# Transposed softmax weights of the first mixer's heads written into the PSUM bank of the small sums

## The chip, the cores and the metric

The kernel runs on one NeuronCore of a Trainium2 chip. The engines that matter are TensorE (PE in the profile; its weight loads have a row of their own, PEld), VectorE (DVE), ScalarE (ACT) and GpSimd (POOL). SyncE (SP) issues nearly all transfers from HBM. The results of TensorE land in PSUM, which has 8 banks of 128 partitions by 512 fp32 values. The metric is device time in microseconds of one execution; lower is better.

## The reference

One inference step of a two-layer diffusion backbone of width 2048 for two groups of 128 tokens: context tokens, and latent tokens that also attend to 128 cached context keys. Layer 0 has a mixer with two kinds of heads side by side, layer 1 another mixer; each is followed by a gated ConvFFN. A modulation vector per group and sub-layer (`silu(cond) @ w_ada`) gives shift, scale and gate. The change lies in layer 0's mixer alone:

```python
def mixer_ab(h, ...):                       # cut to what matters
    proj = h @ w_in
    qb = rmsnorm(8 query heads of 128, g_qn)            # grouped-query heads, 2 key heads
    qa = rmsnorm(q_lat, g_q) @ w_q_up                   # 8 latent heads of 128 + 64
    kv = ckv_all @ w_kv_up                              # their keys and values
    s  = q @ k.T * scale                                # 128 queries x 128 (group i) or 256 (group ii) keys
    out = softmax(s) @ v                                # 16 heads
    return concat(out) @ w_out
```

## The kernel before, in words

All activations stand transposed: features over the 128 partitions, the 256 tokens of both groups along the free axis. Every fp32 product is made exact enough by halves: each weight block is cast to a high half `wh` on ACT (L248), the rest `wl` is subtracted on DVE (L249), and three products (`wh` with the high half of the activations, `wl` with it, `wh` with their low half) are accumulated per block in a bank called `acc`. A product of a weight block therefore waits for its load, its cast and its subtraction.

The 8 banks of PSUM are given out by name: three `acc`; one `ada` for the sums of the modulation; three `att` for the attention; and one `misc` (function `bank`), which holds the small sums of the norms and their spread over the partitions. A name with several banks is a ring: who takes the next one waits until the last reader of its former content is done.

The stage of the heads takes from about 214 to 350 us of the span. It goes through four rounds (the loop over `h`). A round has three products with `w_q_up` (two latent queries, called `qn`, and their rotary part), the norms of two further grouped-query heads (`gqa_query`: a square on ACT, a sum of two 128x1 multiplications into `misc`, `rstd` with DVE L219 and a power on POOL L222, a scale on POOL L1238, a rotation on DVE L858 to L861), two grouped-query heads (`gqa`), two products with `w_kv_up` for keys, the values, and a pair of latent heads (`mla_pair`). Here G0 to G7 are the grouped-query heads and M0 to M7 the latent ones, in the order G0 G1 M0 M1, G2 G3 M2 M3 and so on.

What a head does is in `scores` and `head_ab`: scores into an `att` bank; two maxima on DVE (L867, L868); their negative and its scaling on POOL (L872, L873); two exponentials on ACT (L875), which also give the sums; a reciprocal on DVE (L903) and two multiplications that normalise `p` (L904, L905). Then `transposed`: three transposes of 128x128 on PE into one bank and a copy `pT` on ACT (L884). Then the three products with the values into another `att` bank, which are split in halves into `hx` (ACT L248, DVE L249).

Beside this runs side work for the modulation. `Deep` (L525) multiplies blocks of `w_ada` with the condition on DVE and sums them: two products of 128x1024 for each block, in tiles called `block` and `kvb`, each with a single home, so that the next load (SP L522) starts when the second product of the block before is done. On PE, `sum_rows` sums other blocks (`araw`, two buffers) into `ada`.

The order of the instructions on each engine is not written out. A scheduler lays it out beforehand along a simulated timeline in which waits for banks count; it may put any ready instruction first, other than those that `keep_order` holds in their written order (the side work and some others). So a changed bank can change the order on every engine, and that order is then fixed: an instruction that waits holds all those behind it on its engine.

Of the kernel before, what the change touches and what calls it, by code (L numbers as in the profile page):

```python
# [18 lines left out]
P = 128  # L19
# [75 lines left out]
def step_kernel(ctx: ExitStack, tc: tile.TileContext, A: dict):  # L95
# [34 lines left out]
    ppool = {}  # L130
# [6 lines left out]
    def nm(s):  # L137
        uid[0] += 1
        return f"{s}_{uid[0]}"

    def T_(pl, shape, tag, dt=F32, bufs=None):
        kw = {} if bufs is None else {"bufs": bufs}
        return pl.tile(shape, dt, tag=tag, name=nm(tag), **kw)
# [81 lines left out]
    def bank():  # L225
        return T_(pmisc, [P, 512], "misc")
# [20 lines left out]
    def split(out_hi, out_lo, src, pin=lambda i: i):  # L247
        pin(act.copy(out_hi, src))  # L248
        pin(dve.tensor_tensor(out=out_lo, in0=src, in1=out_hi.bitcast(F32), op=ALU.subtract))  # L249
# [614 lines left out]
    def softmax_parts(s, mx, sums, rs, const, p, pin=lambda i: i):  # L864

        nmx = T_(small, [P, 2], "nmx")
        pin(dve.tensor_reduce(out=mx[:, 0:1], in_=s[:, 0:T], axis=AX.X, op=ALU.max))  # L867
        pin(dve.tensor_reduce(out=mx[:, 1:2], in_=s[:, T:3 * T], axis=AX.X, op=ALU.max))  # L868
        if rs is None:
            pool.tensor_scalar(out=nmx, in0=mx, scalar1=-const, scalar2=None, op0=ALU.mult)  # L870
        else:
            pool.tensor_scalar(out=nmx, in0=mx, scalar1=-1.0, scalar2=None, op0=ALU.mult)  # L872
            pool.tensor_tensor(out=nmx, in0=nmx, in1=rs, op=ALU.mult)  # L873
        for g, c in ((0, slice(0, T)), (1, slice(T, 3 * T))):
            act.activation(p[:, c], s[:, c], AF.Exp, bias=nmx[:, g:g + 1],  # L875
                           scale=const if rs is None else rs[:, g:g + 1],
                           accum_out=sums[:, g:g + 1])

    def transposed(pl, p):
        pt = T_(ppool["att"], [P, 512], "att", bufs=3)  # L880
        for b in range(3):
            pe.transpose(pt[:, b * T:(b + 1) * T], p[:, b * T:(b + 1) * T], ident)
        o = T_(pl, [P, 3 * T], "pT", bufs=2)
        act.copy(o, pt[:, :3 * T])  # L884
        return o
# [10 lines left out]
    def head_ab(pl, s, rs, v, hx, c):  # L896

        mx = T_(small, [P, 2], "mx")
        sums = T_(small, [P, 2], "sums")
        p = T_(pl, [P, 3 * T], "p", bufs=3)  # L900
        softmax_parts(s, mx, sums, rs, None, p)
        rec = T_(small, [P, 2], "rec")
        dve.reciprocal(out=rec, in_=sums)  # L903
        dve.tensor_scalar(out=p[:, :T], in0=p[:, :T], scalar1=rec[:, 0:1], scalar2=None, op0=ALU.mult)  # L904
        dve.tensor_scalar(out=p[:, T:], in0=p[:, T:], scalar1=rec[:, 1:2], scalar2=None, op0=ALU.mult)  # L905
        yield
        yield
        pT = transposed(pl, p)
        yield
        o = T_(ppool["att"], [P, 512], "att", bufs=3)  # L910
        pe.matmul(o[:, 0:T], v(0), pT[:, 0:T], start=True, stop=True)
        pe.matmul(o[:, T:NT], v(1), pT[:, T:2 * T], start=True, stop=False)
        pe.matmul(o[:, T:NT], v(2), pT[:, 2 * T:], start=False, stop=True)
        split(hx[:, c, :NT], hx[:, c, NT:2 * NT], o[:, :NT])


    def mixer_ab(hx, beside):
        l = 0
        with tc.tile_pool(name="ab", bufs=1) as ab:
# [297 lines left out]
            with tc.tile_pool(name="abh", bufs=1) as hp:  # L1217
# [24 lines left out]
                def gqa(h):  # L1242
                    k = kg[:, h // 4]
                    return head_ab(hp, scores(qb[:, h], k), rsb[:, h], lambda b: vg[:, b, h // 4], o, 8 + h)
# [18 lines left out]
                def mla_pair(h, qr, kn, vm):  # L1263
                    s = [T_(ppool["att"], [P, 512], "att", bufs=3) for i in range(2)]
                    for g, ks in KEYS:
                        for i in range(2):
                            pe.matmul(s[i][:, ks], qn[h + i][:, g * T:(g + 1) * T], kn[i][:, ks],
                                      start=True, stop=False)
                        for i in range(2):
                            half = slice(64 * i, 64 * i + 64)  # L1270
                            m = pe.matmul(s[i][:, ks], qr[half, g * T:(g + 1) * T], kr[half, ks],
                                          start=False, stop=True)
                            if i:
                                keep_order(m)
                    for i in range(2):
                        start(head_ab(hp, s[i], rsm, lambda b, i=i: vm[:, b, i], o, h + i))
# [66 lines left out]
    def mixer_c(cp, hx, W, ready, st):  # L1343
# [70 lines left out]
        def attend(h, q, k, v):  # L1414
# [24 lines left out]
            yield  # L1439
            yield  # L1440
            pT = transposed(cp, pj[0])
            yield
            o = T_(ppool["att"], [P, 512], "att", bufs=3)
# [337 lines left out]
```

## Time and profile before

| | |
|---|---|
| time, median of 3 runs | 2304.97 us (2304.84, 2304.97, 2305.27) |
| profiled execution, its span | 2305.7 us (the page gives no other time of it) |
| busy in the whole span | PE 2275.9 us (99%), DVE 1885.6 us (82%), ACT 1195.7 us (52%), POOL 188.1 us (8%) |
| stage of the heads, 214 to 356 us: busy of 142 us | PE 135.66, DVE 114.95, ACT 73.47, POOL 25.90 |
| PE's granted clock in that stage | 0.98 of full speed |

The profiled execution is 0.7 us longer than the median of the timed runs. The page's chain of waits is the work that ended last, followed back from the end of the program; its timelines give each instruction's start and duration and, in brackets, the idle time before it and who ended that. A multiplication of fp32 operands (scores, sums S, sums into `ada`) stands as two records in the profile where the program has one instruction.

### The profile page before, as it was taken

The numbers are of one execution on the slowest core, as the hardware profiler recorded it, in microseconds if no ns is written. First come the engines' busy times: TensorE is split into PE (matmuls) and PEld (weight loads), VectorE is DVE, ScalarE is ACT, GpSimd is POOL, SyncE is SP. The second block draws the span as 40 slices with busy tenths as digits, with TensorE's granted clock in tenths as the row PEclk, the third lists the DMA queues.
The fourth block names the chain that finished last, engine by engine and source line by source line (L and its number), as shares of the span: only waits on it lengthen the run. The fifth ranks groups of instructions, "written<-read, shape, count | busy, mean of one in ns | idle before, by whom it ended". The sixth has DMA issues, their size and how long they took to land.

```text
span 2305.7 us, 47484 instructions
## 1 busy us (share of the span) xinstructions
PE 2275.9 (99%) x19496; PEld 2182.1 (95%) x19496; DVE 1885.6 (82%) x2973; ACT 1195.7 (52%) x1959; POOL 188.1 (8%) x238
## 2 busy tenths in 40 slices
PE   8999999999999999999999999999999999999998
PEld 6788878999999999999999999999999999999998
DVE  4667979989999999999978988898899965666654
ACT  4345555665553355555575455457555434555543
POOL 0002111300000000001130001023000000000011
PEclk9999999999999999999999999999999999999999
DMA  9987888777777777777788888776667755555553
GB/s 376 367 343 293 326 311 338 288 277 264 262 255 291 291 272 260 272 258 258 288 293 293 318 322 310 267 268 229 246 256 262 264 200 189 199 191 194 198 189 126
DMA packets 100122, 617.15 MB, mean 268 GB/s; under 512 B 10752, under 2 KB 18880, under 8 KB 33344
## 3 DMA queue, kind: packets, MB, share of 16 engines
q1 hardware_dynamic: 99904, 614.11, 72.2%
q8 instruction: 153, 2.51, 0.4%
q14 instruction: 65, 0.53, 0.1%
HBM read 609.32 MB, written 4.75 MB: 266 GB/s over the span
## 4 chain that ended last, share of the span: by engine, by line
PE 93%; DVE 3%; DMA 2%; issue 1%; POOL 1%; ACT 1%; SPq 0%; DVEq 0%; ACTq 0%; POOLq 0%
PE acc L110 86%; PE ada L110 3%; PE att L110 2%; DVE wl L249 1%; DVE hx L525 1%; DMA more<-w_ada 1%; PE att L113 1%; DMA raw<-w_out_c 0%; PE misc L110 0%; DMA araw<-w_ada 0%; DMA kvb<-w_ada 0%; POOL dev L807 0%; PE ada L113 0%; DVE rope L858 0%; ACT wh L248 0%
## 5 line engine op out<-in xcount | busy, mean ns | idle before, releaser
L110 PE MATMUL acc<-hx,wh 128*128 128x256 f32 (+1 forms) x7264 | 1255.2, 278 | 4.2 <-ACT wh L248 1.7
L248 ACT CAST wh<-raw 128x1024 fp32r<-128x1024 f32 (+1 forms) x834 | 796.6, 967 | 869.8 <-PE acc L110 736.6
L249 DVE TENSOR_TENSOR wl<-raw,wh 128x1024 fp32r<-128x1024 f32 (+1 forms) x834 | 925.4, 1126 | 246.9 <-ACT wh L248 240.2
L110 PEld LDWEIGHTS acc<-hx,wh 128*128 128x128 f32 x7264 | 1099.8, 188 | 23.2 <-ACT wh L248 8.1
L110 PE MATMUL acc<-hx,wl 128*128 128x256 f32 (+1 forms) x3632 | 1007.8, 278 | 5.3 <-DVE wl L249 5.1
L110 PEld LDWEIGHTS acc<-hx,wl 128*128 128x128 f32 x3632 | 684.5, 188 | 9.5 <-DVE wl L249 6.9
L110 PE MATMUL acc<-g,wh 128*128 128x256 f32 x2816 | 478.8, 276 | 0.0
L110 PEld LDWEIGHTS acc<-g,wh 128*128 128x128 f32 x2816 | 424.0, 188 | 0.0
L110 PE MATMUL acc<-g,wl 128*128 128x256 f32 x1408 | 388.1, 276 | 0.0
L473 DVE CUSTOM_DVE_ANT_0 junk<-araw,condb 128x2048 f32<-128x2048 f32 x128 | 294.4, 2300 | 0.0
L110 PEld LDWEIGHTS acc<-g,wl 128*128 128x128 f32 x1408 | 264.2, 188 | 0.0
L211 POOL TENSOR_TENSOR sqacc<-sqacc,sq 128x256 f32<-128x256 f32 x62 | 71.5, 1154 | 1491.1 <-ACT sq L207 1490.9
L110 PE MATMUL acc<-hxc,wh 128*128 128x256 f32 (+1 forms) x1056 | 189.3, 281 | 0.0
L110 PEld LDWEIGHTS acc<-hxc,wh 128*128 128x128 f32 x1056 | 161.9, 188 | 1.8 <-issue 1.7
L110 PE MATMUL acc<-hxc,wl 128*128 128x256 f32 (+1 forms) x528 | 146.9, 278 | 0.0
L110 PEld LDWEIGHTS acc<-hxc,wl 128*128 128x128 f32 x528 | 99.6, 189 | 0.2
L110 PE MATMUL acc<-wh,hxc 128*128 128x256 f32 (+1 forms) x512 | 95.0, 283 | 0.5 <-DVE nt L818 0.5
L1531 ACT ACTIVATE cv<-acc,convw 128x256 f32<-128x256 f32 x169 | 94.1, 557 | 0.0
L525 DVE CUSTOM_DVE_ANT_0 hx<-block,condb 128x1024 fp32r<-128x1024 f32 x65 | 79.3, 1221 | 7.3 <-DMA block<-w_ada 6.8
L1537 DVE SCALAR_TENSOR_TENSOR cv<-acc,convw,cv 128x254 f32<-128x254 f32 x169 | 81.1, 480 | 3.2
L843 DVE SCALAR_TENSOR_TENSOR x<-acc,mod,x 128x128 f32<-128x128 f32 x190 | 57.3, 344 | 31.6 <-PE acc L110 31.6
L110 PEld LDWEIGHTS acc<-wh,hxc 128*128 128x128 f32 x512 | 79.4, 188 | 3.4 <-issue 2.5
(263 smaller groups left out, 1800.4 us busy)
## 6 DMA issues: line engine op xcount, KB each, us to landing
raw<-w_up SPq DMA_DIRECT2D x176, 1024.0 KB, 4.8
araw<-w_ada SPq DMA_DIRECT2D x136, 1024.0 KB, 6.0
raw<-w_down SPq DMA_DIRECT2D x88, 1024.0 KB, 4.8
raw<-w_in_c SPq DMA_DIRECT2D x48, 1024.0 KB, 6.9
block<-w_ada SPq DMA_DIRECT2D x41, 512.0 KB, 6.8
raw<-w_in_ab SPq DMA_DIRECT2D x18, 1024.0 KB, 9.1
raw<-w_out_ab SPq DMA_DIRECT2D x16, 1024.0 KB, 7.9
raw<-w_out_c SPq DMA_DIRECT2D x16, 1024.0 KB, 7.1
```

Of the source, the lines that this page charges most:

```text
L110: return self.placed(nc.tensor.matmul(*a, **kw))
L113: return self.placed(nc.tensor.transpose(*a, **kw))
L211: eng.tensor_tensor(out=st["acc"], in0=st["acc"], in1=sq, op=ALU.add)
L248: pin(act.copy(out_hi, src))
L249: pin(dve.tensor_tensor(out=out_lo, in0=src, in1=out_hi.bitcast(F32), op=ALU.subtract))
L473: keep_order(dve.tensor_tensor_reduce(out=T_(feat["pool"], [P, D], "junk"), in1=feat["row"][:, c], in0=feat["raw"].rearrange("p g n -> p ( ...
L525: keep_order(dve.tensor_tensor_reduce(out=self.junk, in0=self.raw, in1=self.row[:, c].rearrange("p (g n) -> p g n", g=2), scale=1.0, scala ...
L843: dve.scalar_tensor_tensor(out=x[:, c, s], in0=ps[:, s], scalar=mod[:, l, 3 * which + 2, c, g:g + 1], in1=x[:, c, s], op0=ALU.mult, op1=AL ...
L1531: pin(act.activation(y, ps, AF.Identity, scale=cw[:, 1, m:m + 1], bias=cw[:, 3, m:m + 1]))
L1537: pin(dve.scalar_tensor_tensor(out=y3[:, :, :T - 1], in0=p3[:, :, 1:], scalar=cw[:, 2, m:m + 1], in1=y3[:, :, :T - 1], op0=ALU.mult, op1=A ...
```

## The change

`transposed` takes the function that gives out its bank as an argument. The heads of the first mixer pass `bank`, so that the transposes of all 16 heads go into the single `misc` bank. The second mixer keeps the `att` banks. No instruction is added or removed.

```diff
-    def transposed(pl, p):
-        pt = T_(ppool["att"], [P, 512], "att", bufs=3)
+    def transposed(pl, p, bank=att_bank):
+        pt = bank()
         for b in range(3):
             pe.transpose(pt[:, b * T:(b + 1) * T], p[:, b * T:(b + 1) * T], ident)
         o = T_(pl, [P, 3 * T], "pT", bufs=2)
...
         yield
         yield
-        pT = transposed(pl, p)
+        pT = transposed(pl, p, bank)
         yield
         o = T_(ppool["att"], [P, 512], "att", bufs=3)
```

In the `att` ring each head took three banks before (scores, transposes, outputs) and now takes two. In the `misc` bank the takers now follow one another in this order, where T is a head's transposes and S the sum of a query's norm: T(G0), S(G2), T(G1), T(M0), T(M1), S(G3), T(G2), S(G4), T(G3), T(M2), T(M3), S(G5), T(G4), S(G6), T(G5), T(M4), T(M5), S(G7), T(G6), T(G7), T(M6), T(M7). Each waits for the reader of the one before: the ACT copy after T, the DVE addition (L219) after S.

The scheduler orders the stage anew. Up to about 225 us of the span and from about 360 us on the rows are the same; between them rows move on all engines. Three places follow. The numbers behind the names tell tiles apart.

On PE, the scores of G2 (`att_2921`) and G3 (`att_2983`), with what stands around them. `acc_3164` is a product with `w_q_up`, `acc_3392` one with `w_kv_up` for keys, `acc_3427` one for values, `misc_2963` is S(G3), `att_2887` the output of M1. Before:

```order
L110 MATMUL att_2887<-pT_2848,vm_2663 128x128 x3
L110 MATMUL ada_2731<-araw_2740,condw_79 32x512 x4
L110 MATMUL ada_2731<-araw_2742,condw_79 32x512 x4
L110 MATMUL att_2921<-kg_118,qb_242 128x128
L110 MATMUL att_2921<-kg_118,qb_242 128x256
L110 MATMUL acc_3095<-wh_2944,kv_in_1786 128x256
L110 MATMUL acc_3164<-ql_1787,wh_3156 128x256 x2
L110 MATMUL acc_3164<-ql_1787,wl_3157 128x256
L110 MATMUL acc_3164<-ql_1787,wh_3156 128x256 x2
L110 MATMUL att_2983<-kg_118,qb_242 128x128
```

With the change:

```order
L110 MATMUL att_2887<-pT_2848,vm_2663 128x128 x3
L110 MATMUL ada_2731<-araw_2740,condw_79 32x512 x4
L110 MATMUL ada_2731<-araw_2742,condw_79 32x512 x4
L110 MATMUL att_2921<-kg_118,qb_242 128x128
L110 MATMUL att_2921<-kg_118,qb_242 128x256
L110 MATMUL misc_2963<-cst_74,sq_2918 128x1 x2
L110 MATMUL att_2983<-kg_118,qb_242 128x128
L110 MATMUL att_2983<-kg_118,qb_242 128x256
L110 MATMUL acc_3392<-kv_in_1786,wh_3323 128x384 x2
L110 MATMUL acc_3392<-kv_in_1786,wl_3324 128x384
L110 MATMUL acc_3427<-wh_3327,kv_in_1786 128x256
```

Counted over the whole listing, 55 multiplications of 128x256 into `acc` and 21 of 128x384 more stand ahead of G2's scores than before, and two sums S (of two multiplications each) fewer. Between G2's scores and T(G2) there stood 43 multiplications of 128x256, four transposes and three sums into `ada`, beside both scores; now there stand 24 of 128x256, three of 128x384, four transposes and S(G3).

On DVE, from the maxima of G2 (`mx_2924`). `hx_2383` behind L525 is only where the product of the side work is dropped. Before:

```order
L867 TENSOR_REDUCE mx_2924<-att_2921 128x1
L868 TENSOR_REDUCE mx_2924<-att_2921 128x1
L525 ISA hx_2383,mod_77<-block_2728,condb_1794 128x1024
L525 ISA mod_77 128x1
L249 TENSOR_TENSOR wl_3254<-raw_3247,wh_3253 128x512
L867 TENSOR_REDUCE mx_2986<-att_2983 128x1
L868 TENSOR_REDUCE mx_2986<-att_2983 128x1
L445 TENSOR_REDUCE mod_77<-ada_2911 128x8
L903 RECIPROCAL rec_2934<-sums_2925 128x2
L447 TENSOR_TENSOR mod_77<-mod_77,cst_74 128x8
L904 TENSOR_SCALAR p_2926<-p_2926,rec_2934 128x128
L905 TENSOR_SCALAR p_2926<-p_2926,rec_2934 128x256
```

With the change:

```order
L525 ISA hx_2383,mod_77<-kvb_2804,condb_1794 128x1024
L525 ISA mod_77 128x1
L525 ISA hx_2383,mod_77<-block_2893,condb_1794 128x1024
L525 ISA mod_77 128x1
L867 TENSOR_REDUCE mx_2924<-att_2921 128x1
L868 TENSOR_REDUCE mx_2924<-att_2921 128x1
L219 TENSOR_SCALAR rv_2966<-misc_2963 128x2
L525 ISA hx_2383,mod_77<-block_2893,condb_1794 128x1024
L525 ISA mod_77 128x1
L867 TENSOR_REDUCE mx_2986<-att_2983 128x1
L868 TENSOR_REDUCE mx_2986<-att_2983 128x1
L858 TENSOR_TENSOR rope_3354<-qb_242,cst_74 64x128 x2
```

Behind these rows now come, ahead of `p_2926`, a subtraction `wl_3579` of 128x1024, the reciprocals of G2 and G3 and a few small rows. Ahead of `p_2926` stand in all, beside small rows, four products of L525 more than before (two of `kvb_2804`, two of `block_2893`), three subtractions of 128x1024 (`wl_3324`, `wl_3328`, `wl_3579`), the rotation of a latent query (`rope_3280`, `qr_3278`) and half of a grouped-query head's (`rope_3354`).

On POOL, the last two grouped-query heads, G6 (`nmx_3688`) and G7 (`nmx_3747`); `rr_3729` is the power for the norm of G7. One piece of the difference:

```order
 L872 TENSOR_SCALAR nmx_3688<-mx_3685 128x2
+L222 TENSOR_TENSOR rr_3729<-rv_3727,cst_74 128x2
 L873 TENSOR_TENSOR nmx_3688<-nmx_3688,rsb_122 128x2
+L1238 TENSOR_SCALAR rsb_122<-rr_3729 128x2
 L872 TENSOR_SCALAR nmx_3747<-mx_3744 128x2
 L873 TENSOR_TENSOR nmx_3747<-nmx_3747,rsb_122 128x2
```

The power of a later head's norm now stands between the two POOL steps of G6; G2 (`rr_2968`) and G4 (`rr_3351`) have the same.

## The prediction

> **What bounds the kernel now.** I read the page's busy times and its chain of waits first, then the stage of the heads by windows, then its waits, and last the timelines of PE and DVE in it.
>
> ```profile
> PE 2275.9 (99%) x19496; PEld 2182.1 (95%) x19496; DVE 1885.6 (82%) x2973; ACT 1195.7 (52%) x1959; POOL 188.1 (8%) x238
> PE 93%; DVE 3%; DMA 2%; issue 1%; POOL 1%; ACT 1%; SPq 0%; DVEq 0%; ACTq 0%; POOLq 0%
> ```
>
> TensorE bounds the whole program: its work is the same after the change, so the time can move only by its idle time, and by its clock. The windows show where that is (us, then busy PE, PEld, DVE, ACT, POOL, then granted clock, share of the DMA engines, GB/s):
>
> ```profile
> 214.00:356.00 142.00, 135.66 (x1013) 109.38 (x1012) 114.95 (x286) 73.47 (x180) 25.90 (x48) 0.98 0.83 315
> 245.00:255.00 10.00, 10.00 (x77) 10.00 (x76) 9.74 (x30) 7.66 (x22) 3.72 (x7) 1.00 0.95 392
> 325.00:335.00 10.00, 5.25 (x28) 2.41 (x31) 8.45 (x21) 3.22 (x11) 1.84 (x4) 0.75 0.78 300
> 335.00:345.00 10.00, 10.00 (x73) 7.78 (x66) 5.25 (x16) 3.58 (x8) 0.41 (x2) 0.91 0.70 265
> ```
>
> In the stage that the change touches PE is idle for 142 − 135.66 = 6.3 us, most of it behind 325 us. In 245 to 255 us DVE is busy for 9.74 of 10 us: there VectorE is nearly as full as TensorE, so a DVE row that is moved ahead of a head's softmax delays that softmax by its whole length. The idle time of PE has three places:
>
> ```profile
> 265.37 1.06 PE L110 MATMUL ada<-araw,condw 128*32 128x512 f32 x6 [0.56 <-DVE mod L445]
> 331.88 0.87 PE L113 MATMUL att<-cst,p 128*128 128x128 f32 x3 [4.54 <-DVE p L904]
> 347.09 0.39 PE L110 MATMUL acc<-hx,wl 128*128 128x256 f32 x1 [0.72 <-DVE wl L249]
> ```
>
> The 4.54 us are the last grouped-query heads, G6 and G7: nothing is left to multiply while their softmax runs. No wait of PE in the stage is for a bank of the `att` ring, so the two banks that each head now takes in place of three remove no wait that the trace shows. What the change does comes by the order that the scheduler makes of it.
>
> **G2: two budgets.** Its transposes must wait for a longer chain on DVE, while PE has less to do behind its scores. The prices:
>
> ```profile
> 257.85 0.92 PE L110 MATMUL att<-kg,qb 128*128 128x128 f32 x4
> 258.42 0.47 PE L110 MATMUL acc<-wh,kv_in 128*128 128x256 f32 x1
> 261.01 0.60 PE L113 MATMUL ada<-cst,am 128*128 128x128 f32 x4
> 261.37 0.36 PE L110 MATMUL acc<-ql,wl 128*128 128x256 f32 x1
> 263.29 0.39 PE L110 MATMUL acc<-ql,wh 128*128 128x256 f32 x2
> 263.63 0.39 PE L110 MATMUL acc<-ql,wh 128*128 128x256 f32 x2
> 244.77 0.51 PE L110 MATMUL acc<-kv_in,wh 128*128 128x384 f32 x2
> 245.29 0.51 PE L110 MATMUL acc<-kv_in,wh 128*128 128x384 f32 x2
> 221.06 0.50 PE L110 MATMUL misc<-cst,sq 128*128 128x1 f32 x4
> 221.42 0.36 PE L110 MATMUL att<-kg,qb 128*128 128x128 f32 x1
> ```
>
> Starts follow each other, so a difference of starts is the price: a head's scores 258.42 − 257.85 = 0.57 us; four transposes 0.36; three multiplications of 128x256 0.34, or 0.113 each; three of 128x384 0.52, or 0.173 each; a sum S 0.36. By the count in the order 55 × 0.113 + 21 × 0.173 − 2 × 0.36 = 9.1 us more stand ahead of G2's scores, which then start at 257.85 + 9.1 = 267.0. Behind them come G2's and G3's scores, one S, three of 128x384, 24 of 128x256 and four transposes: 1.14 + 0.36 + 0.52 + 2.71 + 0.36 = 5.1 us. PE is at G2's transposes at 272.1. Before, that stretch was 266.44 − 257.85 = 8.6 us long.
>
> On DVE:
>
> ```profile
> 258.19 0.42 DVE L249 TENSOR_TENSOR hx<-att,hx 128x256 fp32r<-128x256 f32 x1
> 258.53 1.22 DVE L525 CUSTOM_DVE_ANT_0 hx<-kvb,condb 128x1024 fp32r<-128x1024 f32 x1
> 261.18 1.23 DVE L525 CUSTOM_DVE_ANT_0 hx<-block,condb 128x1024 fp32r<-128x1024 f32 x1 [1.09 <-DMA block<-w_ada]
> 262.86 1.22 DVE L525 CUSTOM_DVE_ANT_0 hx<-block,condb 128x1024 fp32r<-128x1024 f32 x1
> 264.00 0.69 DVE L249 TENSOR_TENSOR wl<-raw,wh 128x512 fp32r<-128x512 f32 x1
> 264.60 0.29 DVE L867 TENSOR_REDUCE mx<-att 128x1 f32<-128x128 f32 x1
> 265.13 0.18 DVE L445 TENSOR_REDUCE mod<-ada 128x8 f32<-128x32 f32 x1
> 265.90 0.17 DVE L903 RECIPROCAL rec<-sums 128x2 f32<-128x2 f32 x1 [0.58 <-ACT p L875]
> 266.10 0.29 DVE L904 TENSOR_SCALAR p<-p,rec 128x128 f32<-128x128 f32 x1
> 267.71 1.22 DVE L249 TENSOR_TENSOR wl<-raw,wh 128x1024 fp32r<-128x1024 f32 x1
> 268.85 1.22 DVE L525 CUSTOM_DVE_ANT_0 hx<-kvb,condb 128x1024 fp32r<-128x1024 f32 x1
> 248.44 1.17 DVE L858 TENSOR_TENSOR rope<-nt,cst 32x128 f32<-32x128 f32 x4
> DMA to landing us min/median/max: 4.1/6.7/11.3
> ```
>
> A product of the side work costs 264.00 − 262.86 = 1.14 us, a subtraction of 128x1024 as much (268.85 − 267.71), one of 128x512 0.60. Ahead of G2's normalisation now stand four products (4.6), three subtractions (3.4), a latent query's rotation (1.17 and two rows of some 0.2: 1.5) and half of a head's (estimated 0.8 from the same row): 10.3 us more. The order could use the 1.09 and 0.58 us that DVE waited here before. By load alone it is at that row at 266.10 + 10.3 − 1.7 = 274.7, and PE goes on at about 274.9: a wait of **2.8 us**, the lower bound.
>
> The transfer makes it longer. The second product of `block_2728` ended at 264.0; ahead of it now stand 0.60 + 2 × 1.14 and the 1.5 of the rotation, while a pair of maxima (265.13 − 264.60 = 0.53) and two splits of outputs (258.53 − 258.19 = 0.34 each) have gone behind: 264.0 + 4.4 − 1.2 = 267.2. Only then can the next block be loaded; the last row above gives 4.1 us at least and 6.7 at the median from issue to landing. With the first product of that block (1.14) ahead of G2's maxima these start at 272.4, or 275.0. From there to the normalised weights DVE has two pairs of maxima (1.06), a product, a subtraction, the half rotation and small rows: 1.06 + 1.14 + 1.14 + 0.8 and, for the small ones, about 1.0, or 5.1 us. That is 277.5 or 280.1, a wait of 5.4 or 8.0 us. I take **+4.0**, nearer to the load than to the median transfer, since DVE's being 3 us late is itself worked out and its waits would let part of it catch up.
>
> **G4.** Here 12 multiplications of 128x256, eight sums into `ada`, two pairs of scores and one S are left to PE between scores and transposes.
>
> ```profile
> 322.09 1.92 PE L110 MATMUL ada<-araw,condw 128*32 128x512 f32 x16
> 332.68 3.64 PE L110 MATMUL ada<-araw,condw 128*32 128x512 f32 x16
> L222 POOL TENSOR_TENSOR rr<-rv,cst x8: 707/1010/1760, 215.6 to 305.6; 128x2 f32<-128x2 f32 x8
> ```
>
> That is 1.36 + 1.92 + 1.14 + 0.36 = 4.8 us. On DVE its scores (0.57) are followed by two pairs of maxima, two products, half a rotation and small rows, 0.57 + 1.06 + 2.28 + 0.6 + 0.6 = 5.1, and on POOL a power of 0.71 to 1.76 us now stands between the two steps of its scaling; together 5.6 to 6.9. I take **+1.2** (0 to 2.1).
>
> **The end: G6 and G7.** The 4.54 us wait has a late transfer in it:
>
> ```profile
> 323.53 1.23 DVE L525 CUSTOM_DVE_ANT_0 hx<-kvb,condb 128x1024 fp32r<-128x1024 f32 x1 [2.53 <-DMA kvb<-w_ada]
> 325.39 0.82 PE L110 MATMUL att<-kg,qb 128*128 128x128 f32 x4
> 327.75 0.29 DVE L867 TENSOR_REDUCE mx<-att 128x1 f32<-128x128 f32 x1
> 328.83 1.26 POOL L873 TENSOR_TENSOR nmx<-nmx,rsb 128x2 f32<-128x2 f32 x1
> ```
>
> DVE stood 2.53 us for `kvb` and reached G6's maxima at 327.75, 1.8 us after their scores were done (325.39 + 0.57). If PE comes later by the waits above, the transfer is no longer late: −1.5 (0 to −1.8). Against it S(G7) has moved in (0.36 on PE, and there it fills a wait) with its power between G6's two POOL steps: +1.0 (0.7 to 1.76). Together **−0.5**.
>
> **The single bank itself.** Each transpose now waits for the copy of the one before, within a pair of latent heads above all:
>
> ```profile
> L884 ACT COPY pT<-att x16: 478/479/511, 231.7 to 352.8; 128x384 f32<-128x384 f32 x16
> ```
>
> In three of the four pairs at least a dozen multiplications stand between the two, over 1.3 us against 0.48. In the pair M4 and M5 nothing does: **+0.5**.
>
> The Trainium skill, "Perfetto Trace Analysis", section "Optimizing Tensor Performance", says that independent groups of products should rotate through different PSUM banks, so that one's evacuation overlaps the next one's products. By it all 16 transposes would pay the copy, 16 × 0.48 = 7.7 us; the order lets one in 16 pay, and no run here shows the other yet.
>
> **Small waits of before.** The 0.56 at 265.37 goes, as the sums that waited are moved: **−0.6**. The 0.72 at 347.09 goes, since the exponentials of M6 and M7 now stand ahead of fewer casts and their transposes are spread: **−0.7**.
>
> **The clock.** After the 4.54 us wait the same 16 sums took 3.64 in place of 1.92 us, and the windows show 0.75 and 0.91: 1.7 us of half clock. A new wait of 4 us at G2 can bring this once more, a shorter one at the end can save it. Net **0**, bounds ±1.7. The Trainium skill, "TensorE: Matmul & The Clock Gate", section "HAM oscillation — how this bites in real kernels", puts the limit at idle gaps of about 3.4 us; the clock here agrees for 4.54 us, and by the page the 4.0 us at G2 would be just enough for the +1.7.
>
> **Sum.** 4.0 + 1.2 − 0.5 + 0.5 − 0.6 − 0.7 + 0 = +3.9 us. The profiled execution's span is 2305.7, 0.7 above the median of 2304.97; I take the difference from one to the other as unchanged, so 2304.97 + 3.9 = **2308.9 us**. The bounds of the terms give 2.8 + 0 − 1.1 + 0.5 − 1.3 − 1.7 = −0.8 and 8.0 + 2.1 + 1.8 + 0.5 − 1.3 + 1.7 = +12.8.
>
> **Rivals.** *DVE catches up* (chance 0.25). Side work that went ahead of G2 isn't to be done later, and where the waits for `block` (1.09) shrink the new waits are 1.5 us at G2 and 0.5 at G4: 1.5 + 0.5 − 0.5 + 0.5 − 1.3 = +0.7, about 2305.7. For it: DVE has 142 − 115 = 27 us of idle time in the stage. Against it: almost none of that lies around 245 to 255.
>
> *The end closes* (chance 0.13), on the other side: with PE shifted later, DVE has done its side work when G6's scores come, and S(G7) and its power fall into time that was idle anyway. Of the 4.54 us at most 1.5 stay, its half clock is saved, and G2's wait is a short one of 1.0 as DVE catches up: 1.0 − 3.0 − 1.7 − 1.3 + 0.5 = −4.5, and −6.0 where nothing stays: 2299.0 to 2300.5. It decides once the wait before G6's transposes falls below 1.5 us. For it speaks the 2.53 us for `kvb`, against it that the power now stands in G6's own chain.
>
> *Waits add up* (chance 0.12): the median transfer holds G2 by 8.0, G4 pays 2.1 and half clock comes twice: 8.0 + 2.1 − 0.5 + 0.5 − 1.3 + 1.7 = +10.5, 2313 to 2317. For it: DVE's 9.74 of 10 us; against it: the least of the landing times is 2.6 us shorter.
>
> *No change at all* is no rival here: the rows of four engines differ.
>
> **How the numbers follow.** The forecast has 0.50 with an own range of 2306.5 to 2311.5. A measurement of this kernel can tell from no change about 0.2%, 4.6 us: 2300.4 and 2309.6 are the edges. Of the forecast's 0.50, 0.28 lie below 2309.6 and 0.22 above; DVE's catching up is all "same"; of the closing end 0.10 is faster and 0.03 same; the sum of waits is slower. That makes 0.10 faster, 0.56 same, 0.34 slower. The range of 2302 to 2314.5 leaves out most of the closing end and half of the sum of waits, some 0.16.
>
> **What would show it.** In the changed profile PE should wait for `DVE p L904` ahead of G2's transposes (now into `misc`) by 2.8 to 5.4 us, around 272 us, with DVE busy before it and a wait for `block` or none; G4's by about 1 us; the wait before G6's near 4 us. If PE waits there for ACT's copy in more than one pair, the bank term is wrong; if G2's wait is below 2 us, the DVE budget is; if the stage behind 325 us still shows a clock of 0.75 and G2 another one, the clock term is. A change outside 225 to 360 us would make the whole frame wrong.

## The result, and the profile after

The change made the kernel slower: 2311.63 us median of six runs (2309.27 to 2315.09) against 2305.32 us of the kernel before; ratio 1.0027, 95% interval 1.0017 to 1.0037. On a second chip it was 2312.37 us against 2305.74, ratio 1.0030 (1.0019 to 1.0041). The predicted time was 2308.9 us, the range 2302 to 2314.5.

The page of the profiled execution (its time was 2310.14 us), the span, the busy times and the chain of waits:

```profile
span 2308.4 us, 47487 instructions
PE 2271.7 (98%) x19496; PEld 2179.4 (94%) x19496; DVE 1886.3 (82%) x2973; ACT 1196.0 (52%) x1959; POOL 189.6 (8%) x238
PE 91%; DVE 3%; DMA 3%; POOL 1%; issue 1%; ACT 1%; SPq 0%; DVEq 0%; ACTq 0%
```

TensorE does the same work and stands idle for longer. Where this lies is read between two instructions that both kernels have: the first scores of G0, and, behind the heads, the second of two rows of eight records each of sums into `ada`. I call the time between them the stage. Before, then with the change, from the timelines of PE:

```profile
218.32 0.38 PE L110 MATMUL att<-kg,qb 128*128 128x128 f32 x2
...
367.29 1.06 PE L110 MATMUL ada<-araw,condw 128*32 128x512 f32 x8
```

```profile
216.32 0.38 PE L110 MATMUL att<-kg,qb 128*128 128x128 f32 x2
...
370.13 1.07 PE L110 MATMUL ada<-araw,condw 128*32 128x512 f32 x8
```

The stage took 148.97 us and takes 153.81, so +4.8; in the second chip's profile of the change it took 154.92. From its end to the end of the program both take 1938.3 to 1938.4 us, so all of the loss is here. It began 2 us earlier in the changed kernel's profile: earlier in the program, where both have the same rows, the clock granted to PE differed from one execution to the other (0.83 in two windows of 10 us from 70 to 90 us before, 1.00 after). That is why the two spans differ by only 2.7 us, and why one span alone would mislead here. The span is also not the time: here it is 2308.4 us of 2310.14, so 2305.7 us of span before belong to a time of about 2307.5 (an estimate by the same difference), some 2.5 above the median and not 0.7.

The waits of PE in the stage, in its timeline (start, duration, instruction, in brackets the idle time before it and who ended that):

```profile
252.67 0.50 PE L110 MATMUL acc<-ql,wh 128*128 128x256 f32 x2 [1.30 <-ACT vm L1258]
272.39 0.39 PE L110 MATMUL acc<-wh,kv_in 128*128 128x256 f32 x1 [1.17 <-ACT vm L1258]
274.60 0.61 PE L113 MATMUL misc<-cst,p 128*128 128x128 f32 x3 [0.53 <-DVE p L904]
307.66 0.60 PE L113 MATMUL misc<-cst,p 128*128 128x128 f32 x3 [0.95 <-DVE p L904]
308.88 0.38 PE L110 MATMUL acc<-wh,kv_in 128*128 128x256 f32 x1 [0.62 <-ACT vm L1258]
313.96 0.94 PE L110 MATMUL att<-pT,vg 128*128 128x128 f32 x6 [0.21 <-ACT pT L884]
325.55 0.55 PE L113 MATMUL misc<-cst,p 128*128 128x128 f32 x3 [0.62 <-ACT pT L884]
335.59 0.87 PE L113 MATMUL misc<-cst,p 128*128 128x128 f32 x3 [4.34 <-DVE p L904]
358.08 0.84 PE L110 MATMUL acc<-hx,wh 128*128 128x256 f32 x4 [0.46 <-ACT hx L248]
```

They sum to 10.2 us; before they were 0.56 + 0.21 + 4.54 + 0.72 = 6.0. That is +4.2 of the +4.8. Only 0.62 us of it is a wait for the single bank (the copy `pT` of the head before, M4, ahead of M5's transposes). The largest new part, 1.30 + 1.17 + 0.62 = 3.1 us, is a wait that the prediction did not have at all: for the copy `vm` of the values, which frees an `acc` bank. Why that copy is late shows on ACT, at a latent head of the first round and at a grouped-query head of the third (the first and the last of the three waits):

```profile
251.25 0.46 ACT L875 ACTIVATE p<-att,nmx,rsmla 128x128 f32<-128x128 f32 x1 [1.39 <-POOL nmx L873]
251.71 0.55 ACT L875 ACTIVATE p<-att,nmx,rsmla 128x256 f32<-128x256 f32 x1
252.25 0.91 ACT L1258 COPY vm<-acc 128x256 f32<-128x256 f32 x3
...
307.47 0.46 ACT L875 ACTIVATE p<-att,nmx,rsb 128x128 f32<-128x128 f32 x1 [2.39 <-POOL nmx L873]
307.92 0.56 ACT L875 ACTIVATE p<-att,nmx,rsb 128x256 f32<-128x256 f32 x1
308.46 0.37 ACT L1258 COPY vm<-acc 128x256 f32<-128x256 f32 x1
```

and at G2, on ACT, POOL and DVE:

```profile
268.21 0.28 DVE L867 TENSOR_REDUCE mx<-att 128x1 f32<-128x128 f32 x1
268.81 1.22 DVE L525 CUSTOM_DVE_ANT_0 hx<-block,condb 128x1024 fp32r<-128x1024 f32 x1
268.98 1.11 POOL L872 TENSOR_SCALAR nmx<-mx 128x2 f32<-128x2 f32 x1 [17.76 <-DVE rv L219]
269.22 1.05 ACT L248 CAST wh<-raw 128x1024 fp32r<-128x1024 f32 x1 [0.16 <-PE acc L110]
270.06 0.71 POOL L222 TENSOR_TENSOR rr<-rv,cst 128x2 f32<-128x2 f32 x1
270.73 0.21 POOL L873 TENSOR_TENSOR nmx<-nmx,rsb 128x2 f32<-128x2 f32 x1
270.98 0.46 ACT L875 ACTIVATE p<-att,nmx,rsb 128x128 f32<-128x128 f32 x1 [0.70 <-POOL nmx L873]
271.43 0.56 ACT L875 ACTIVATE p<-att,nmx,rsb 128x256 f32<-128x256 f32 x1
271.97 0.37 ACT L1258 COPY vm<-acc 128x256 f32<-128x256 f32 x1
```

On ACT the copy `vm` stands behind G2's two exponentials. These wait for POOL's scaling of the maxima. Its first step, on 128x2 numbers, takes 1.11 us, where the same step takes 0.21 with nothing beside it on DVE: here it runs beside a product of the side work (268.81 to 269.95) and ends just behind it. Then the power for G3's norm takes another 0.71. ACT had a cast until 270.27, so 0.70 us of POOL's delay reach it, and the two exponentials take 1.0 more. So ACT leaves an `acc` bank full, and PE stands still, with other work behind in its queue. The copy came at 271.97, and PE went on at 272.39.

The slow step on POOL is not new. Before, at G2:

```profile
258.93 0.37 ACT L1258 COPY vm<-acc 128x256 f32<-128x256 f32 x1 [0.35 <-PE acc L110]
263.10 1.05 POOL L872 TENSOR_SCALAR nmx<-mx 128x2 f32<-128x2 f32 x1 [6.11 <-DVE mx L868]
264.78 0.46 ACT L875 ACTIVATE p<-att,nmx,rsb 128x128 f32<-128x128 f32 x1 [4.96 <-POOL nmx L873]
```

It took 1.05 us there, and the 32 scaling steps of the stage's heads take 14.3 us in all in both profiles. ACT stood idle for 4.96 us, and PE did not stop for it: the copy of the values had gone ahead of the exponentials. What the change made new is the place of that copy, behind the exponentials.

### The profile page after: what moved, and what is told of

It is laid out like the page before. It is cut to its first block, busy times and chain, and to the rows that moved or that the text cites. A ratio compares the mean times of both kernels' runs of the same rounds, so it can differ in the third digit from the quotient of the medians.

```text
span 2308.4 us, 47487 instructions
## 1 busy us (share of the span) xinstructions
PE 2271.7 (98%) x19496; PEld 2179.4 (94%) x19496; DVE 1886.3 (82%) x2973; ACT 1196.0 (52%) x1959; POOL 189.6 (8%) x238
## 4 chain that ended last, share of the span: by engine, by line
PE 91%; DVE 3%; DMA 3%; POOL 1%; issue 1%; ACT 1%; SPq 0%; DVEq 0%; ACTq 0%
PE acc L110 85%; PE ada L110 3%; PE att L110 2%; DVE hx L525 1%; DVE wl L249 1%; DMA more<-w_ada 1%; DMA block<-w_ada 1%; DMA raw<-w_in_ab 1%; DMA raw<-w_out_c 0%; DMA araw<-w_ada 0%; PE misc L110 0%; POOL dev L807 0%; ACT wh L248 0%; PE ada L113 0%; PE att L113 0%
## 5 line engine op out<-in xcount | busy, mean ns | idle before, releaser
L525 DVE CUSTOM_DVE_ANT_0 hx<-block,condb 128x1024 fp32r<-128x1024 f32 x65 | 79.3, 1220 | 8.6 <-DMA block<-w_ada 5.2
```

Of the source, the lines that this page charges most:

```text
L525: keep_order(dve.tensor_tensor_reduce(out=self.junk, in0=self.raw, in1=self.row[:, c].rearrange("p (g n) -> p g n", g=2), scale=1.0, scala ...
```

## The experiments

In each table row "stage" is the time between the two instructions above, in the one profiled execution; the timed ratio is against the kernel before on the same chip.

| kernel | median us | before us | ratio (95% interval) | stage us | last wait (G6) us |
|---|---|---|---|---|---|
| before | | | | 148.97 | 4.54 |
| the change | 2311.63 | 2305.32 | 1.0027 (1.0017 to 1.0037) | 153.81 | 4.34 |
| the change, second chip | 2312.37 | 2305.74 | 1.0030 (1.0019 to 1.0041) | 154.92 | 4.34 |
| latent heads alone | 2306.67 | 2306.06 | 1.0004 (0.9996 to 1.0013) | 150.67 | 4.51 |
| grouped-query heads alone | 2308.27 | 2306.06 | 1.0014 (1.0005 to 1.0023) | 153.30 | 3.07 |
| sums in `acc` | 2308.51 | 2305.74 | 1.0014 (1.0006 to 1.0023) | 150.46 | 4.32 |
| values copied by DVE | 2322.89 | 2305.74 | 1.0072 (1.0059 to 1.0085) | 164.73 | 5.99 |
| scaling on DVE, on the change | 2306.26 | 2306.06 | 1.0002 (0.9993 to 1.0010) | 147.38 | 2.71 |
| scaling on DVE, on before | 2307.53 | 2306.06 | 1.0004 (0.9995 to 1.0013) | 150.23 | 4.43 |
| sums in `acc`, scaling on DVE | 2306.07 | 2305.74 | 1.0001 (0.9992 to 1.0010) | 150.48 | 4.34 |
| scaling on ACT, on the change | 2304.18 | 2305.27 | 0.9996 (0.9987 to 1.0005) | 147.96 | 3.18 |
| scaling on ACT, on before | 2305.91 | 2305.27 | 1.0003 (0.9994 to 1.0012) | 149.96 | 4.39 |
| sums in `acc`, scaling on ACT | 2306.99 | 2305.27 | 1.0010 (1.0001 to 1.0019) | 151.31 | 4.42 |
| side products out of the stage | 2374.68 | 2305.15 | 1.0300 (1.0286 to 1.0315) | 145.53 | 2.64 |

**The change again.** The same kernel, on the chip of three of the runs below (`vm` copied by DVE, sums in `acc` with and without the scaling on DVE):

> The change itself once more, beside the experiments on one chip. If the first comparison (2311.6 against 2305.3 us) holds on another chip: 2309 to 2313 us against 2306, and the stage of the heads 3.5 to 5.5 us longer than before. If that was the chip or a few unlucky runs: below 2309 us.

2312.37 us: the loss is real and not of one chip. The profile has the same waits as the first, with 1.44 in place of 1.30 at the first `vm`.

**Which heads.** `head_ab` gets the bank as an argument; the change's bank goes to the latent heads alone, or to the grouped-query heads alone:

```diff
-    def head_ab(pl, s, rs, v, hx, c):
+    def head_ab(pl, s, rs, v, hx, c, bank=att_bank):
...
-                        start(head_ab(hp, s[i], rsm, lambda b, i=i: vm[:, b, i], o, h + i))
+                        start(head_ab(hp, s[i], rsm, lambda b, i=i: vm[:, b, i], o, h + i, bank))
```

> Only the eight latent heads put their transposes into the misc bank; the grouped-query heads keep the att ring. Theory A (the loss comes with the new order: the scores of the grouped-query heads come late, their exponentials stand on ScalarE ahead of the copies of the values, and TensorE waits for an acc bank): here the grouped-query heads keep an order close to the one before, so no wait for the values' copy at G2 or G4, and 2304 to 2307 us. Theory B (the single bank itself: each taker waits for the reader of the one before): the pairs of latent heads follow each other directly in the bank, so about half of the loss stays, 2308 us or more, with waits of PE for the copy pT.

> Only the eight grouped-query heads put their transposes into the misc bank, where they alternate with the sums of the norms. Theory A: the order is the change's, the copies of the values stand behind the exponentials again, waits for them of 2 us or more in all, 2309 to 2314 us. Theory B: half of the transposes in the bank, half of the loss, about 2308 us, and no wait for a copy pT within a pair.

With the latent heads alone the time is that of before within the measurement (2306.67 against 2306.06), although their pairs are the ones that follow each other in the bank. With the grouped-query heads alone it is 2308.27, a third to a half of the loss; no wait for `vm` of 2 us came (1.3 in all), and the time lies just below what theory A expected: it is the one that theory B gave for this run. In its profile, at G4:

```profile
305.54 0.70 PE L113 MATMUL misc<-cst,p 128*128 128x128 f32 x3 [1.31 <-DVE p L904]
306.78 0.58 PE L110 MATMUL acc<-wh,kv_in 128*128 128x256 f32 x1 [0.53 <-ACT vm L1258]
```

The pairs of latent heads in the bank cost nothing that the times show, so theory B falls for them. What loss the halves show comes with the heads whose transposes alternate with the sums of the norms; whether by the order or by the bank this run does not tell. The longest wait for `vm` of the change, 1.30 us behind a latent head, is in neither half. And half and half do not add up to the whole (0.0004 + 0.0014 against 0.0027), as each version is laid out anew.

**Sums out of the bank.** In the change, only the sum of a query's norm goes elsewhere:

```diff
-                    pst = T_(pmisc, [P, 512], "misc")
+                    pst = T_(pacc, [P, 512], "acc")
```

> The change, with the sums of the queries' norms in an acc bank, so that the misc bank holds transposes alone. Theory A (the loss comes from the alternation of transposes and sums in one bank, which puts the next head's transposes behind a sum, its reader and the copy, and so the order): the grouped-query exponentials come back ahead of the values' copies or far from them; no wait for those copies over 0.5 us; 2304 to 2307 us. Theory B (the single bank for 16 transposes): no change from the change's 2309 to 2312 us.

2308.51 us and a stage of 150.46: over half of the loss is gone, and no wait for `vm` is left, as theory A has it; the time is above its 2304 to 2307 and below theory B's 2309. The misc bank now holds transposes alone, all 16 of them, and the wait for `pT` is 0.15 us. What is left of the loss in the timed runs (+2.8 us) is more than the stage shows in its one profile (+1.5).

**Values copied by another engine.** To take the copy `vm` out of ACT's queue:

```diff
-                        act.copy(vm[:, b].rearrange("p i d -> p (i d)"), ps[:, :2 * P])
+                        dve.tensor_copy(vm[:, b].rearrange("p i d -> p (i d)"), ps[:, :2 * P])
```

> The change, with the copies of the values out of the acc banks (12 of 128x256) made by VectorE in place of ScalarE. Theory A1 (ScalarE's queue: in the change 1.30, 1.17 and 0.62 us of PE's waits were for these copies behind an exponential that waited for POOL): these waits go, some 3 us, less up to 1 for the added VectorE work: 2307 to 2310 us. Theory A2 (the late scores of the grouped-query heads themselves, whatever engine then waits): the time only moves to waits for the normalised p, 2310 to 2313 us.

Neither theory expected this: 2322.89 us. PE then waited for the copies on DVE, 9.5 us in four waits, the longest two of 4.6 and 3.85. From its profile, DVE and PE:

```profile
250.82 1.23 DVE L525 CUSTOM_DVE_ANT_0 hx<-block,condb 128x1024 fp32r<-128x1024 f32 x1 [2.83 <-DMA block<-w_ada]
...
253.23 1.22 DVE L525 CUSTOM_DVE_ANT_0 hx<-block,condb 128x1024 fp32r<-128x1024 f32 x1
254.58 1.22 DVE L249 TENSOR_TENSOR wl<-raw,wh 128x1024 fp32r<-128x1024 f32 x1
255.71 0.42 DVE L1258 COPY vm<-acc 128x256 f32<-128x256 f32 x1
```

```profile
256.18 0.80 PE L110 MATMUL acc<-ql,wh 128*128 128x256 f32 x2 [3.85 <-DVE vm L1258]
```

A copy of 0.42 us stood behind a product that waited 2.83 us for a transfer of the side work. Whoever drains a bank of PE must not stand in a queue in which something waits for a transfer. As a test between A1 and A2 it says nothing, since it put in a worse wait than the one it took out.

**The scaling of the maxima without POOL.** In the change, and in the kernel before, the two POOL steps become one DVE instruction:

```diff
-            pool.tensor_scalar(out=nmx, in0=mx, scalar1=-1.0, scalar2=None, op0=ALU.mult)
-            pool.tensor_tensor(out=nmx, in0=nmx, in1=rs, op=ALU.mult)
+            dve.scalar_tensor_tensor(out=nmx, in0=mx, scalar=-1.0, in1=rs,
+                                     op0=ALU.mult, op1=ALU.mult)
```

> The change, with the two POOL steps of each head's scaling (negate, multiply) replaced by one DVE instruction on 128x2. In the change POOL's first step took 1.11 us at G2, 1.17 at G3, each about as long as the DVE product beside it, and a power of 0.71 stood between the steps. Theory A (the chain maxima, POOL, exponential, and what ScalarE holds behind it): the exponentials start 1 to 2 us earlier, the waits at G2 and G4 (1.7 and 1.6 us in the change) fall below 1 together, the last wait falls from 4.3 to 2.5 to 3 us and its half clock goes: 2304 to 2307 us. Theory B (the bank): no less than 2309 us.

> The kernel before with the same replacement. If POOL's steps are on the chain of the last grouped-query heads (0.21, 1.26 and the steps between in 4.54 us), the last wait falls to about 2.7 us and its half clock goes: 2301 to 2303 us. If they are hidden there, 2305 us.

With the sums of the queries' norms in an `acc` bank as well:

> Both repairs on the change: sums in an acc bank, and the scaling of the maxima by one VectorE instruction. If the two are independent, the waits of the middle of the stage go with the first and 1.5 to 2 us of the last wait with its half clock go with the second: 2301 to 2304 us, better than both kernels. If the last wait is set by something else (the single-head softmax chain of maxima, exponentials, normalisation): 2305 us.

On the change the loss is gone: 2306.26 us, stage 147.38. On before it gained nothing. First PE's waits in the change with the new scaling, then DVE's rows at the end in before with it:

```profile
303.42 0.39 PE L110 MATMUL acc<-wh,kv_in 128*128 128x256 f32 x1 [1.72 <-ACT vm L1258]
...
330.89 0.61 PE L113 MATMUL misc<-cst,p 128*128 128x128 f32 x3 [2.71 <-DVE p L904]
331.43 1.92 PE L110 MATMUL ada<-araw,condw 128*32 128x512 f32 x16
```

```profile
330.51 0.28 DVE L867 TENSOR_REDUCE mx<-att 128x1 f32<-128x128 f32 x1
330.70 0.42 DVE L868 TENSOR_REDUCE mx<-att 128x1 f32<-128x256 f32 x1
331.04 1.22 DVE L525 CUSTOM_DVE_ANT_0 hx<-block,condb 128x1024 fp32r<-128x1024 f32 x1
332.17 0.23 DVE L872 SCALAR_TENSOR_TENSOR nmx<-mx,rsb 128x2 f32<-128x2 f32 x2
```

In the change the last wait falls to 2.71 us and no half clock follows (16 records of sums in 1.92). The waits for `vm` went only in part. Those of the first round and of G2 are gone, but at G4 the 0.62 us became 1.72 and 0.26, behind exponentials that now waited for DVE; expected was less than 1 us at G2 and G4 together. In before the order puts a side product of 1.14 us between the maxima and their scaling, so the last wait stays at 4.43: what was waited for on POOL is now waited for on DVE.

**The scaling on ACT.** Two Identity activations on 128x1 ahead of the exponentials, with a negated scale that POOL makes beforehand:

```diff
-            pool.tensor_scalar(out=nmx, in0=mx, scalar1=-1.0, scalar2=None, op0=ALU.mult)
-            pool.tensor_tensor(out=nmx, in0=nmx, in1=rs, op=ALU.mult)
+            for g in range(2): act.activation(nmx[:, g:g + 1], mx[:, g:g + 1], AF.Identity, scale=rs[1][:, g:g + 1])
+            rs = rs[0]
```

> The change, with the scaling of the maxima on ScalarE itself, just ahead of the exponentials that use it (two Identity activations on 128x1, with a negated copy of the scale that POOL makes beforehand). Now neither POOL (whose small step took 1.1 us beside a VectorE product of 1.14 us) nor a VectorE product stands between maxima and exponentials. Theory C (those steps set the waits of the change): waits in the middle of the stage under 1.5 us in all, the last wait about 3 us (2 maxima, two products of the side work, exponentials), no half clock behind it: 2303 to 2306 us, as with the scaling on VectorE or better. If the late scores alone are the cause: 2309 us or more.

> The kernel before, with the same scaling on ScalarE. With it on VectorE a product of the side work (1.14 us) stood between maxima and scaling, and the last wait stayed at 4.43 us. Here it can't: last wait 3 to 3.5 us, half clock mostly gone, 2302 to 2304 us; but a load of ScalarE's table now stands in that chain, and if it takes over 1 us the wait stays at 4 to 4.5 and the time at 2305 to 2307 us.

> The change with sums of the queries' norms in an acc bank and the scaling on ScalarE. If both kinds of delay are gone: waits of the middle under 1 us, last wait about 3 us, 2301 to 2304 us, faster than both kernels. If the last wait again is over 4 us: 2305 us.

On the change: 2304.18 us, the lowest median of all, though not told from the kernel before (0.9987 to 1.0005). The waits for `vm` fall to 0.7 us in all, the last wait of the stage to 3.18. On before: 2305.91, since the table load that was named as the risk stands in the chain of G6:

```profile
325.74 0.57 ACT L872 ACTIVATE nmx<-mx,nrsb 128x1 f32<-128x1 f32 x2 [1.65 <-DVE mx L867]
326.33 1.28 ACT L875 ACT_TABLE_LOAD   x1
327.62 0.46 ACT L875 ACTIVATE p<-att,nmx,rsb 128x128 f32<-128x128 f32 x1
```

The two pairs also answer whether the bank itself costs anything: with the scaling on DVE the change is at 2306.26 and before at 2307.53; with it on ACT, 2304.18 and 2305.91. Where POOL is out of the chain the same edit is not slower (the intervals against the kernel before overlap, so no gain is shown either). The two repairs do not add: with the sums in `acc` as well it is 2306.07 (scaling on DVE) and 2306.99 (on ACT), because the last wait is again 4.34 and 4.42 us: side products stand once more between the heads' maxima, reciprocal and normalisation.

**Side products out of the stage.** The suspected root taken away, in the change. Nothing is left out; the products are made in the stage behind:

```diff
-SIDE = {"in3": 0.4, "heads": 1.6, "out0": 1.8, "c": 2.2, "outc": 2.0}
+SIDE = {"in3": 0.4, "heads": 0.0, "out0": 1.8, "c": 2.2, "outc": 2.0}
```

> The change, without the side products of the modulation (L525) on VectorE during the heads after the first round's start; they are made in the stage behind, so the whole time can be longer, and the stage of the heads from the first scores of the grouped-query heads to the second sum into ada behind it is what counts (149.0 us before, 153.8 and 154.9 in two profiles of the change). If those products are what delays the softmax (POOL's step held beside them, maxima and normalisation queued behind them): waits in the middle under 1 us in all, POOL's first step back to about 0.2 us, the last wait 2 to 3 us, the stage 146 to 149 us. If the late scores and the single bank set the waits: 152 us or more.

The stage takes 145.53 us with all 16 transposes in the one bank. Between the two anchors PE waits 0.48 us once in the middle and 2.64 at the end; it waits neither for `vm`, nor for `pT`, nor for a sum. From the timelines of PE and POOL, and the group of POOL's first step (min, median and max in ns):

```profile
327.89 0.88 PE L113 MATMUL misc<-cst,p 128*128 128x128 f32 x3 [2.64 <-DVE p L904]
328.70 3.08 PE L110 MATMUL ada<-araw,condw 128*32 128x512 f32 x16
```

```profile
325.05 0.21 POOL L872 TENSOR_SCALAR nmx<-mx 128x2 f32<-128x2 f32 x1 [10.90 <-DVE rv L219]
```

```profile
L872 POOL TENSOR_SCALAR nmx<-mx x16: 214/214/1122, 222.0 to 339.4; 128x2 f32<-128x2 f32 x16
```

At G6, where POOL's first step took 1.11 us in the change, it takes 0.21. The whole time is 2374.7 us: the products then pile up behind, where PE is busy for only 3 and 5 tenths of two slices of the page (about 415 to 534 us). So moving them there costs far more than it saves; and they are what makes the softmaxes of this stage late. The kernel before was not run without them, so this run shows that the single bank alone sets no long wait, not that the two kernels would then be equal.

## Why the prediction was right or wrong

The sign and the range were right: slower, 2311.6 in 2302 to 2314.5. The forecast of +3.9 us was too small (the measured loss is 6.3, the interval of the ratio +3.9 to +8.5 us), and 0.56 of the chance lay on "same" against 0.34 on "slower". That the sum came near is partly luck: its largest term, the wait at G2, was nearly absent, and waits that were not in the sum took its place.

- **The frame** held: all of the difference lies between the two anchors, and most of it is idle time of PE. The single bank was rightly taken as a small term: +0.5 predicted at M5, 0.62 measured there. The rule that was weighed against it (the Trainium skill, "Perfetto Trace Analysis", section "Optimizing Tensor Performance": rotate independent groups through banks) did not decide; one head's transposes in 16 paid for the copy.
- **G2 is the step that failed, on PE's side.** The predicted wait of 4.0 us for the normalised weights was 0.53. All times here are counted from the stage's start, which lies at 218.32 us before and 216.32 after. The prediction let PE run without a stop to G2's transposes and be there at 53.8; it was there at 57.75, since it had stood 1.30 and 1.17 us for `vm` on the way (the other 1.5 us are not taken apart). DVE was as late as foretold: the weights came at 57.85, by the sum at 56.4 (load alone) or 59.2 (with the transfer). So the short wait does not mean that DVE caught up, as the prediction's own sign would have it; PE came late too, and went on at 58.3, against 57.8 in the forecast. In the DVE budget the transfer was too dear: the second product of `block_2728` ended at 46.6 and not at 48.9, so G2's maxima came at 51.9 and not at 54.1. Behind them DVE waited 1.22 us for the exponentials, a wait that the sum did not have:

```profile
274.02 0.17 DVE L903 RECIPROCAL rec<-sums 128x2 f32<-128x2 f32 x1 [1.22 <-ACT p L875]
274.17 0.28 DVE L904 TENSOR_SCALAR p<-p,rec 128x128 f32<-128x128 f32 x1
```

- **What stood in its place, 3.1 us, was not in the sum:** PE's waits for `vm`. The prediction followed DVE and PE and took ACT (52% busy) as a carrier of latency only; it never read what the new order put behind the exponentials on ACT. With the change each of the three waits is for a copy that stands right behind an exponential on ACT, and before each of these exponentials ACT waited for POOL (1.39, 0.70 and 2.39 us).
- **G4**: +1.2 predicted; 0.95 for the weights and 0.62 for `vm`. The term was right for the weights.
- **The end**: −0.5 predicted, −0.4 measured (4.34 and no 0.21, against 4.54 + 0.21), with both parts there, but smaller: DVE's wait for `kvb` shrank from 2.53 to 0.85 us, and POOL's power moved in and took 0.70. POOL's two scaling steps took 1.11 and 0.19, against 0.21 and 1.26 before, so the slow one only changed its place.
- **Small waits**: −1.3 predicted; both went, but a new one of 0.46 (358.08) came: −0.8.
- **The clock**: 0 predicted. In the profiles the 16 records of sums (eight sums) behind the last wait took 3.12 us against 3.64. But the changed kernel's runs scatter over 5.8 us (2309.27 to 2315.09), and go with the clock: 0.996 in the three below 2311.2, 0.993 in the two above 2313.9. The timed loss (6.3 and 6.6) is larger than the stage's in one profile (4.8 and 5.9).

Of the stage's +4.8 us, 4.2 are waits and about −0.5 clock; some 1.1 us more, in multiplications that were not idle, I did not trace. A part of it may lie in the stops themselves: before the wait of 1.17 us the last multiplication starts at 270.93 and the next at 272.39, 1.46 us apart where 0.11 is usual, so this stop costs 1.35 and not 1.17. There are five more stops than before; at 0.2 each, an estimate from this one, that is 1.0. What was shown: with POOL out of the scaling the change's loss is gone in the timed runs, with the sums out of the bank half of it or more; with the side products out it is gone in the stage. What was only argued: that the loss comes by the order alone. Every edit is laid out anew by the scheduler, so no run changed the bank with the order held.

The rivals: DVE did not catch up, though G2's wait of 0.53 looks like it, and the time did not fall; the end did not close, its wait stayed over 4 us; the waits did not add up through transfers.

## What to carry to other kernels

In an order fixed beforehand, read for each engine what the new order queues *behind* a waiting instruction, and above all behind which exponential or transfer a copy stands that empties a PSUM bank: an engine at half load can stop TensorE that way. A slow step that was harmless can become dear without being any slower, once such a copy stands behind it. A short wait need not mean that the late engine caught up: look whether the waiting engine came late too. A small bank shared by two uses costs little by its own waits (0.6 us here); that it costs more by the order that it forces is what these runs suggest. A side job that fills an engine's gaps should not be able to stand inside another engine's chain of small steps.

## What the runs showed of the hardware

A POOL step on 128x2 numbers took 0.21 us alone and 1.11 or 1.17 us beside a DVE instruction with two operands of 128x1024, ending 0.1 us behind it:

```profile
331.68 1.22 DVE L525 CUSTOM_DVE_ANT_0 hx<-block,condb 128x1024 fp32r<-128x1024 f32 x1
331.86 1.11 POOL L872 TENSOR_SCALAR nmx<-mx 128x2 f32<-128x2 f32 x1 [8.80 <-DVE rv L219]
```

The Trainium skill, "SBUF — State Buffer", section "SBUF: two separate sides", states that VectorE and GpSimd share a port pair as an exclusive lock that the first holds for its whole instruction, while the other is fully blocked; a VectorE instruction with two inputs in SBUF takes it against a GpSimd instruction that reads SBUF. The rows agree. The profile of before has it as well: the POOL step at 328.83, which I had quoted, took 1.26 us, and I had not asked what ran beside it on DVE (a product from 328.82).

The half clock did not follow the length of the wait alone: behind 2.64 us (side products out) the 16 records took 3.08, behind 2.71 us (scaling on DVE) 1.92, behind 3.07 us (grouped-query heads alone) 3.64. Behind the same 4.34 us they took 3.12 in one profile of the change and 3.64 in the other. The Trainium skill, "TensorE: Matmul & The Clock Gate", section "What's actually happening", describes a window of about 3.4 us that runs freely; that the phase counts would fit these figures, but no run here tells it apart, and the 2.64 us of idle time are shorter than the one idle window that the page names.
